# Gate and up of the second layer's FFNs as seven half-size products in place of eight, in three feature groups with partial sums in DRAM

## The chip, the cores and the metric

The kernel runs on one core of one Trainium2 chip. The metric is the device time of one execution in microseconds (us). Engines are named as the profile names them: PE does matrix products (PEld is its weight load), DVE elementwise work, ACT activations, casts and copies, POOL elementwise work and some DMA issues, SP all other DMA issues. Each engine takes its instructions in the order in which the built program has them.

## The reference

Two layers run over 640 tokens of 1024 features (128 of a context, 512 latents), all in float32. A layer is an FFN, a mixer (attention, RG-LRU and S5 branches), and a second FFN, each between two norms whose scale and shift come from a condition (the adaLN vectors):

```python
def _swiglu(h, wg, wu, wd):
    return (jax.nn.silu(h @ wg) * (h @ wu)) @ wd

def _layer(x, mod, lp, ctx):
    s0, c0, g0, s1, c1, g1, s2, c2, g2 = jnp.split(mod, N_MOD, axis=-1)
    h = _rms(x, lp["g_pre"][0]) * (1 + c0) + s0
    f = _swiglu(h, lp["w_ffn_gate"][0], lp["w_ffn_up"][0], lp["w_ffn_down"][0])
    x = x + 0.5 * g0 * _rms(f, lp["g_post"][0])
    ...
    h = _rms(x, lp["g_pre"][2]) * (1 + c2) + s2
    f = _swiglu(h, lp["w_ffn_gate"][1], lp["w_ffn_up"][1], lp["w_ffn_down"][1])
    x = x + 0.5 * g2 * _rms(f, lp["g_post"][2])
```

D_FF is 2816. So an FFN's gate and its up are each a product of 640 x 1024 by 1024 x 2816, its down one of 640 x 2816 by 2816 x 1024. mod = silu(c) @ w_mod + b_mod has 72 blocks of 128 values for a layer and for each of the two conditions.

## The kernel before

The two layers have four FFNs; in the order of the program they are the first and second (layer 0) and the third and fourth (layer 1). Features lie on the partitions for gate and up: a block of 128 features is one step j of 22.

A float32 product is made of three passes over exact parts (`mm3`): the high part of the weights by the high part of the tokens (L93), high by low (L94), low by high (L95). Weights come from DRAM as slabs of 128 x 1024 (`slab`, tile raw, issued by SP). Each half slab is split (`split`): ACT casts it to the high part (L100, tile whi) and DVE subtracts that from the source for the low part (L101, tile wlo). Six such pairs are buffered ahead of PE.

For step j, gate and up each are 8 blocks of the contraction by 3 passes, over 384 tokens and then over 256. Then ACT takes tanh (L433), DVE makes two products out of SBUF and PSUM (L434, L435), and the result is split into the hidden pair (tiles P). After 11 steps (half of the features) down runs over what is there: for each half of the output features, 11 half slabs by 5 token tiles by 3 passes of 512 columns. The first half's sums stay in SBUF (tile part); the second half adds them.

Beside gate and up lies background work at fixed slots of the steps (`plan`, `background`). In the first and the second FFN there are steps that prepare the S5 matrices: the same complex products run on DVE and on POOL (`cmul`, L516 to L524). In all four there are blocks of the adaLN vectors (`mod_tile`): SP brings 128 x 1024 of w_mod, and DVE multiplies and sums it with the two conditions, in halves of 512 columns (L255), with a small sum behind each pair (L258). The first and the third FFN carry 48 such blocks each, the second 24, the fourth 8.

At the end of an FFN each token tile (128 tokens, t = 0 to 4) gets its post norm, its residual and the next pre norm (`post`, `prenorm`). The next norm's scale row is applied before the transposes by DVE (L313, left half) and by ACT and POOL (L314, L315, right half). Then PE transposes (L327), and ACT and DVE add the shift and split (L331 to L338). The tiles 3 and 4 are turned while PE is in the first products of the next phase, which run on the tokens of the tiles 0 to 2.

SP's order is written out in the code; the order on the other engines is set at build time by a scheduler that simulates the program.

## Time and profile before

| | us |
|---|---|
| time, median of 3 runs | 3231.84 (3231.64 to 3232.34) |
| the profiled execution, from first to last instruction | 3232.8 |
| PE busy | 3119.7 (97%) |
| DVE busy | 2008.7 (62%) |
| ACT busy | 1243.2 (38%) |
| POOL busy | 659.9 (20%) |

The profiled execution was taken by itself. Its span is 1.0 us longer than the median of the timed runs, so a time that is worked out within it is compared with the runs by taking 1.0 us off. A busy time is the union of an engine's instructions. PE's matrix products overlap in the records, so the rate of PE is read from the distance between the starts of consecutive ones, not from their lengths. The third FFN runs from about 1664 us to 2112 us of the span, the fourth from about 2756 us to the end.

### The profile page before, as it was taken

What the parts mean: (1) busy time and instruction counts of PE and PEld (TensorE: products, weight loads), DVE (VectorE), ACT (ScalarE), POOL (GpSimd) and SP (SyncE); (2) the same over time, 40 slices, a digit from 0 to 9 for tenths busy, and PEclk for the clock granted to TensorE, in tenths of its full rate; (3) what the DMA queues carried; (4) which work ended last, traced back from release to release, by engine and by line L of the source; (5) the groups of instructions that cost most, each with busy time, mean ns of one, the idle gap of its engine ahead of it and who ended that gap; (6) DMA issues with size and microseconds to landing.
All of it is one profiled execution on the core that took longest, in us unless ns stands there. A gap on an engine that the chain in (4) does not pass through costs nothing.

```text
span 3232.8 us, 52042 instructions
## 1 busy us (share of the span) xinstructions
PE 3119.7 (97%) x19981; PEld 2912.7 (90%) x19981; DVE 2008.7 (62%) x4548; ACT 1243.2 (38%) x2757; POOL 659.9 (20%) x933
## 2 busy tenths in 40 slices
PE   8899999998999999999999999999989999999998
...
GB/s 240 114 181 175 157 157 162 80 80 58 97 140 83 116 133 118 196 98 144 142 152 176 125 112 162 156 113 85 63 67 115 133 72 133 155 85 85 86 98 86
DMA packets 138106, 398.45 MB, mean 123 GB/s; under 512 B 34704, under 2 KB 43424, under 8 KB 135424
## 3 DMA queue, kind: packets, MB, share of 16 engines
...
q10 hardware_dynamic: 720, 1.31, 0.1%
...
HBM read 355.77 MB, written 44.40 MB: 124 GB/s over the span
## 4 chain that ended last, share of the span: by engine, by line
PE 79%; DVE 9%; POOL 6%; issue 3%; ACT 1%; DMA 1%; SPq 0%; POOLq 0%; DVEq 0%; ACTq 0%
PE mm L93 24%; PE mm L94 24%; PE mm L95 24%; POOL s5t L1018 1%; POOL H L1020 1%; POOL s5t L1017 1%; POOL s5t L1019 1%; DVE wlo L101 1%; DVE junk L255 1%; PE mm L1252 1%; DVE x L387 1%; PE mm L1241 1%; PE mm L990 1%; ACT n L310 1%; PE mm L1216 1%
## 5 line engine op out<-in xcount | busy, mean ns | idle before, releaser
L94 PE MATMUL mm<-h,whi 128*128 128x384 f32 (+1 forms) x3968 | 1228.5, 310 | 8.4 <-DVE s L296 5.8
L95 PE MATMUL mm<-h,wlo 128*128 128x384 f32 (+1 forms) x3968 | 1227.2, 310 | 5.8 <-DVE wlo L101 5.8
L93 PE MATMUL mm<-h,whi 128*128 128x384 f32 (+1 forms) x3968 | 1226.2, 311 | 4.5 <-ACT h L337 2.7
L101 DVE TENSOR_TENSOR wlo<-raw,whi 128x512 fp32r<-128x512 f32 x780 | 570.0, 734 | 530.0 <-ACT whi L100 522.6
L94 PEld LDWEIGHTS mm<-h,whi 128*128 128x128 f32 x3968 | 755.9, 191 | 11.4 <-DVE s L296 6.5
L100 ACT CAST whi<-raw 128x512 fp32r<-128x512 f32 x780 | 476.8, 619 | 747.2 <-PE mm L95 367.8
L95 PEld LDWEIGHTS mm<-h,wlo 128*128 128x128 f32 x3968 | 755.7, 191 | 6.9 <-DVE wlo L101 6.8
L93 PEld LDWEIGHTS mm<-h,whi 128*128 128x128 f32 x3968 | 753.9, 191 | 8.7 <-ACT h L337 3.5
L93 PE MATMUL mm<-whi,P 128*128 128x512 f32 x980 | 381.7, 391 | 1.7 <-DVE tmp L434 1.7
L94 PE MATMUL mm<-wlo,P 128*128 128x512 f32 x980 | 381.7, 390 | 0.0
L95 PE MATMUL mm<-whi,P 128*128 128x512 f32 x980 | 381.1, 390 | 0.0
L255 DVE SCALAR_TENSOR_TENSOR junk<-wmod,W 128x512 bf16<-128x512 f32 x512 | 357.7, 699 | 10.3 <-DMA wmod<-w_mod 4.4
L281 POOL DMA_DIRECT2D gd<-grow x6 | 3.2, 528 | 1498.1 <-ACT grow L279 1257.7
L100 ACT CAST P<-tmp 128x384 fp32r<-128x384 f32 x192 | 88.2, 460 | 437.2 <-DVE tmp L435 435.5
L93 PEld LDWEIGHTS mm<-whi,P 128*128 128x128 f32 x980 | 184.0, 188 | 40.4 <-DVE tmp L434 2.2
L95 PEld LDWEIGHTS mm<-whi,P 128*128 128x128 f32 x980 | 184.0, 188 | 38.2
L94 PEld LDWEIGHTS mm<-wlo,P 128*128 128x128 f32 x980 | 184.0, 188 | 37.6
L433 ACT ACTIVATE tmp<-mm 128x384 f32<-128x384 f32 (+1 forms) x176 | 76.4, 435 | 219.8 <-PE mm L95 219.6
L95 PE MATMUL mm<-P,wlo 128*128 128x384 f32 (+1 forms) x512 | 158.8, 310 | 0.0
L94 PE MATMUL mm<-P,whi 128*128 128x384 f32 (+1 forms) x512 | 158.1, 309 | 0.0
L93 PE MATMUL mm<-P,whi 128*128 128x384 f32 (+1 forms) x512 | 158.0, 309 | 0.0
L817 DVE SCALAR_TENSOR_TENSOR tmp<-tmp,mm 128x384 f32<-128x384 f32 x64 | 31.0, 484 | 187.1 <-PE mm L95 94.8
(333 smaller groups left out, 4047.4 us busy)
## 6 DMA issues: line engine op xcount, KB each, us to landing
wmod<-w_mod SPq DMA_DIRECT2D x128, 512.0 KB, 3.6
raw<-w_gate SPq DMA_DIRECT2D x88, 512.0 KB, 3.6
raw<-w_up SPq DMA_DIRECT2D x88, 512.0 KB, 3.6
raw<-w_down SPq DMA_DIRECT2D x88, 512.0 KB, 3.6
raw<-w_in_fm SPq DMA_DIRECT2D x72, 512.0 KB, 3.5
xd<-x SPq DMA_DIRECT2D x25, 512.0 KB, 2.9
x<-xd SPq DMA_DIRECT2D x24, 512.0 KB, 4.5
...
```

What stands on the lines that cost most here:

```text
L93: nc.tensor.matmul(ps, whi, ahi, start=first, stop=False)
L94: nc.tensor.matmul(ps, whi, alo, start=False, stop=False)
L95: nc.tensor.matmul(ps, wlo, ahi, start=False, stop=last)
L100: nc.scalar.copy(hi, src)
L101: return nc.vector.tensor_tensor(lo, src, hi.bitcast(F32), ALU.subtract)
L255: nc.vector.scalar_tensor_tensor(out=jk, in0=w[:, h * 512:(h + 1) * 512], scalar=1.0, in1=rows[c][h], op0=ALU.mult, op1=ALU.mult, accum_ou ...
L310: nc.scalar.activation(n, x, AF.Square, scale=1.0 / 32.0, accum_out=ss)
L387: nc.vector.scalar_tensor_tensor(out=x[:, hs], in0=f[h], scalar=rs, in1=x[:, hs], op0=ALU.mult, op1=ALU.add)
L433: nc.scalar.activation(t, pg[:, :n], AF.Tanh, scale=0.5)
L990: nc.tensor.matmul(pv[:, g], m1[:, g, ri], U[:, 4 * i + g], start=True, stop=True)
L1017: v.tensor_tensor(t[:, 0, :ns], cur, ar, ALU.mult)
L1018: v.tensor_tensor(t[:, 1, :ns], cur[:, :, ::-1], ai, ALU.mult)
```

## The change

In the third and the fourth FFN (`PAIRED`), gate and up work on pairs of steps. Weights of 1024 x 256 are taken as 2 x 2 blocks of 512 x 128, and tokens as two halves of 320 (`TH`). Eight products of half the size become seven (`seven`), with sums of weight blocks, of token blocks and of results in their place:

- Weights: POOL makes four sums of 128 x 512 for a pair and for gate or up (L596). Each of the seven operands is split by ACT and DVE, where four half slabs were split before.
- Tokens: seven operands, kept for the whole FFN in wide tiles (`new_hT`), made once at the boundary before the FFN (`combine`, L364 to L370). The tiles 0, 1 and the first half of 2 give the first two operands; the rest goes into the other five.
- Results: each product of 128 x 320 is copied out of PSUM by ACT or added by DVE (L614, L622, L626, L629, L632). The gate and up values then lie in SBUF, so that DVE's products (L576, L579) have both inputs in SBUF.

A pair of steps has seven products for gate and seven for up. Each is 4 blocks of the contraction by 3 passes over 320 tokens.

The wide tiles take the room in which the hidden pairs and the partial sums lay. So the second, third and fourth FFNs run in three feature groups (`PHASES`), of 6, 8 and 8 steps in the two last. ACT copies a group's down sums out (`put`), and a DMA from POOL's queue writes them to DRAM or adds them there; before the last group's end they are read back (`pd`).

In all FFNs `mod_tile` now sums 1024 columns at once, with one small sum for both conditions. The pre norm's scale is applied with its shift, per feature, after the transposes (`turn`), so POOL has no part in the pre norm any more. The tokens of the condition are computed once.

```diff
-NC_ = 2
-JC = 11
+
+PHASES = {(0, 0): (11, 11), (0, 1): (8, 6, 8), (1, 0): (6, 8, 8), (1, 1): (6, 8, 8)}
+PAIRED = ((1, 0), (1, 1))
+TH = 320
...
-        self.wp = pool("wp", 3)
+        self.wp = pool("wp", 7)
...
-        acc = self.S_(4)
+        m = self.mod[l]["mm"][:, :, col]
         for c in range(2):
-            for h in range(2):
-                jk = self.sm.tile([P, 512], BF16, tag="junk", name=self.nm("junk"), bufs=1)
-                nc.vector.scalar_tensor_tensor(out=jk, in0=w[:, h * 512:(h + 1) * 512], scalar=1.0,
-                                               in1=rows[c][h], op0=ALU.mult, op1=ALU.mult,
-                                               accum_out=acc[:, 2 * c + h:2 * c + h + 1])
-            nc.vector.scalar_tensor_tensor(out=self.mod[l]["m"][c][:, col:col + 1], in0=acc[:, 2 * c:2 * c + 1],
-                                           scalar=acc[:, 2 * c + 1:2 * c + 2], in1=self.mod[l]["b"][:, col:col + 1],
-                                           op0=ALU.add, op1=ALU.add)
...
         rs = self.rstd(ss)
-        self.norm = (
...
-        self.last_n = nc.gpsimd.tensor_tensor(n[:, 512:], n[:, 512:], R["A"][ci][1], ALU.mult)
-        self.turn(t, n, R, hT)
-
...
+    def turn(self, t, n, R, hT):
...
+            for i in range(4):
+                nc.tensor.transpose(ps[:, i * P:(i + 1) * P], n[:, (4 * q + i) * P:(4 * q + i + 1) * P], self.ident)
+            h = n[:, q * 512:(q + 1) * 512].rearrange("p (k t) -> p k t", k=4)
+            for i in range(4):
+                k = slice(4 * q + i, 4 * q + i + 1)
+                o = ps[:, i * P:(i + 1) * P]
+                if i % 2:
+                    v.tensor_scalar(h[:, i], o, a[:, k], b[:, k], ALU.mult, ALU.add)
+                else:
+                    nc.scalar.activation(h[:, i], o, AF.Identity, scale=a[:, k], bias=b[:, k])
+            hs.append(h)
+        if hT.paired:
+            for c, n_, half, o in self.PIECES[t]:
+                d = self.combine(hT, [h[:, :, c:c + n_] for h in hs], half, slice(o, o + n_))
...
+    def combine(self, hT, hs, half, cs):
+        nc, v, g = self.nc, self.nc.vector, self.nc.gpsimd
+        T = {k: (z[:, 0, :, cs], z[:, 1, :, cs]) for k, z in hT.t.items()}
+        if half == 0:
+            self.split(*T["B11"], hs[0])
+            return self.split(*T["B21"], hs[1])
+        h12, h22 = hs
+        n = cs.stop - cs.start
+        f = lambda x: x.bitcast(F32)
+        t1, u = tl(), tl()
+        v.tensor_tensor(t1, f(T["B11"][0]), h12, ALU.subtract)
+        v.tensor_tensor(t1, t1, f(T["B11"][1]), ALU.add)
+        v.tensor_tensor(u, t1, h22, ALU.add)
+        self.split(*T["T1"], t1)
+        g.tensor_tensor(h12, h22, h12, ALU.subtract)
+        g.tensor_tensor(t1, u, f(T["B21"][0]), ALU.subtract)
+        g.tensor_tensor(t1, t1, f(T["B21"][1]), ALU.subtract)
+        self.split(*T["T3"], h12)
+        self.split(*T["T2"], u, -1.0)
+        self.split(*T["B22"], h22)
+        return self.split(*T["T4"], t1)
...
+            h.t = {k: self.wp.tile([P, 2, 4, TH], F32R, tag="W", name=self.nm("h" + k))
+                   for k in ("B11", "B21", "T1", "T3", "T2", "B22", "T4")}
...
+        for ch, n in enumerate(phases):
+            hid = [next(hidden) for _ in range(n)]
...
+                    elif dram:
+                        self.put(t, nh, ps[t], ch)
+                    else:
+                        nc.scalar.copy(part[t][nh], ps[t])
...
+    def put(self, t, nh, ps, ch):
+        nc = self.nc
+        k = (5 * nh + t) % 4
+        o = (self.xp if k % 2 else self.bg).tile([P, 512], F32, tag="x" if k % 2 else "bg", name=self.nm("put"))
+        nc.scalar.copy(o, ps)
+        d = self.pd[t][:, nh * 512:nh * 512 + 512]
+        if ch:
+            nc.gpsimd.dma_start(d, o, accum_op=ALU.add)
+        else:
+            nc.gpsimd.dma_start(d, o)
...
+    def paired(self, l, i, hT):
...
+        big = self.big.tile([P, 5120], F32, tag="big", name=self.nm("raw2"))
+        sets = [[big[:, o:o + 1024], big[:, o + 1024:o + 2048], big[:, o + 2048:o + 2560]] for o in (0, 2560)]
...
+                if jp == 0 and m == 0:
+                    for x in range(2):
+                        ahead[0, x] = opened(0, x)
+                    self.flush()
+                    with ExitStack() as es:
+                        for x in self.norm:
+                            es.enter_context(self.tc.issue_after(x.ins))
+                        ahead[1, 0] = opened(1, 0, True)
+                g, out = ahead.pop((jp, m), None) or opened(jp, m)
+                for done in g:
+                    for f, h in done:
+                        z = out[f][:, h * TH:(h + 1) * TH]
+                        if m == 0:
+                            t = self.tmp.tile([P, 512], F32, tag="tmp", name=self.nm("tmp"))[:, :TH]
+                            nc.scalar.activation(t, z, AF.Tanh, scale=-0.5 if f else 0.5)
+                            v.scalar_tensor_tensor(out=z, in0=t, scalar=1.0, in1=z, op0=ALU.add, op1=ALU.mult)
+                        else:
+                            y = gate[f][:, h * TH:(h + 1) * TH]
+                            v.scalar_tensor_tensor(out=z, in0=z, scalar=0.5, in1=y, op0=ALU.mult, op1=ALU.mult)
+                            self.prod = self.split(*(x[:, h * TH:(h + 1) * TH] for x in hid[f]), z)
+                if m == 0:
+                    gate = out
+                self.background(4 * jp + 2 * m + 1)
+            yield hid[0]
+            yield hid[1]
+
+    def seven(self, src, st, T, out):
+        nc, v, g = self.nc, self.nc.vector, self.nc.gpsimd
+        x, y, s = st
+        nc.sync.dma_start(x, src[:, :1024])
+        self.last_slab = nc.sync.dma_start(y, src[:, 1024:])
+        a11, a12, a21, a22 = x[:, :512], x[:, 512:], y[:, :512], y[:, 512:]
+        add = lambda o, a, b: g.tensor_tensor(o, a, b, ALU.add)
+        o = [[z[:, h * TH:(h + 1) * TH] for h in range(2)] for z in out]
+
+        def product(ps, a, b, more=False):
+            whi, wlo = self.parts(a)
+            for k in range(4):
+                cs = slice(k * P, (k + 1) * P)
+                for e, (w, z) in enumerate(((whi, 0), (whi, 1), (wlo, 0))):
+                    nc.tensor.matmul(ps[:, :TH], w[:, cs], T[b][:, z, k], start=not more and k == e == 0,
+                                     stop=k == 3 and e == 2, skip_group_check=more)
+
+        add(s, a21, a22)
+        add(a21, a21, a11)
+        pa, pb = self.mm(), self.mm()
+        product(pa, a11, "B11")
+        nc.scalar.copy(o[0][0], pa[:, :TH])
+        add(a11, s, a11)
+        product(pb, a12, "B21")
+        v.tensor_tensor(o[0][0], o[0][0], pb[:, :TH], ALU.add)
+        add(a12, a11, a12)
+        yield out
+        yield [(0, 0)]
+        pe, pf = self.mm(), self.mm()
+        product(pe, s, "T1")
+        nc.scalar.copy(o[1][1], pe[:, :TH])
+        product(pf, a21, "T3")
+        v.tensor_tensor(o[1][1], o[1][1], pf[:, :TH], ALU.add)
+        product(pa, a11, "T2", True)
+        nc.scalar.copy(o[0][1], pa[:, :TH])
+        nc.scalar.copy(o[1][0], pa[:, :TH])
+        v.tensor_tensor(o[1][1], o[1][1], pa[:, :TH], ALU.add)
+        yield [(1, 1)]
+        product(pe, a12, "B22", True)
+        v.tensor_tensor(o[0][1], o[0][1], pe[:, :TH], ALU.add)
+        yield [(0, 1)]
+        product(pf, a22, "T4", True)
+        v.tensor_tensor(o[1][0], o[1][0], pf[:, :TH], ALU.add)
+        yield [(1, 0)]
```

The order of instructions shows three places. The first is DVE within the third FFN. Before, in its second half (wlo: the low part of a half slab; tmp: gate or up values, with mm in PSUM; junk: a block of the adaLN vectors):

```order
L435 SCALAR_TENSOR_TENSOR tmp_19941<-tmp_19941,mm_19916 128x256
L258 SCALAR_TENSOR_TENSOR mod_175<-s_19802,bmod_168 128x1
L101 TENSOR_TENSOR wlo_20140<-raw_20133,whi_20139 128x512
L101 TENSOR_TENSOR P_19834<-tmp_19941,P_19833 128x256
L255 SCALAR_TENSOR_TENSOR junk_19950,s_19949<-wmod_19947,W_17541 128x512
L255 SCALAR_TENSOR_TENSOR junk_19952,s_19949<-wmod_19947,W_17541 128x512
L258 SCALAR_TENSOR_TENSOR mod_174<-s_19949,bmod_168 128x1
L255 SCALAR_TENSOR_TENSOR junk_19955,s_19949<-wmod_19947,W_17541 128x512
L434 SCALAR_TENSOR_TENSOR tmp_20045<-tmp_20045,mm_19995 128x384
L255 SCALAR_TENSOR_TENSOR junk_19957,s_19949<-wmod_19947,W_17541 128x512
L258 SCALAR_TENSOR_TENSOR mod_175<-s_19949,bmod_168 128x1
L255 SCALAR_TENSOR_TENSOR junk_19963,s_19962<-wmod_19960,W_17541 128x512
```

After, in its second group of steps (raw_2662: sums of weight blocks; P: gate and up values in SBUF, and their low parts):

```order
L254 SCALAR_TENSOR_TENSOR junk_18760,mod_175<-wmod_18758,srows 128x1024
L579 SCALAR_TENSOR_TENSOR P_18772<-P_18772,P_18613 128x320
L105 TENSOR_TENSOR wlo_18985<-raw_2662_16951,whi_18984 128x512
L254 SCALAR_TENSOR_TENSOR junk_18762,mod_175<-wmod_18758,srows 128x1024
L105 TENSOR_TENSOR wlo_19002<-raw_2662_16951,whi_19001 128x512
L254 SCALAR_TENSOR_TENSOR junk_18767,mod_175<-wmod_18765,srows 128x1024
L254 SCALAR_TENSOR_TENSOR junk_18769,mod_175<-wmod_18765,srows 128x1024
L105 TENSOR_TENSOR wlo_19019<-raw_2662_16951,whi_19018 128x512
L105 TENSOR_TENSOR P_18610<-P_18772,P_18609 128x320
L622 TENSOR_TENSOR P_18773<-P_18773,mm_18820 128x320
L256 TENSOR_TENSOR mod_175<-mod_175,bmod_169 128x2
L105 TENSOR_TENSOR wlo_19041<-raw_2662_16951,whi_19040 128x512
```

Where two splits, a product and a few sums of the adaLN vectors stood between each other, there is now a split at nearly every second place, sums over 1024 columns, and products with both inputs in SBUF. From the first to the last split of this group's weights DVE has 56 splits, 33 additions out of PSUM, 36 products and splits of 320 columns, 24 sums over 1024 columns and 10 small sums; for the third group it is 56, 33, 36, 26 and 11; in the fourth FFN 56, 36, 40, 4 and 2 for either.

The second place is POOL at the start of the third FFN. Before, its last instructions of the norms and then those of the next boundary (s: a norm's root; x: the residual; gd, W: rows of the next boundary):

```order
L300 TENSOR_TENSOR s_17267<-s_17265,mhalf 128x1
L300 TENSOR_TENSOR s_17304<-s_17302,mhalf 128x1
L315 TENSOR_TENSOR n_17262<-n_17262,W_16745 128x512
L390 TENSOR_TENSOR x_17300<-part_14453,x_17300 128x512
L300 TENSOR_TENSOR s_17315<-s_17313,mhalf 128x1
L315 TENSOR_TENSOR n_17310<-n_17310,W_16745 128x512
L281 DMA gd_21509<-grow_21507 32x128
L287 DMA W_21511<-gd_21509 128x2048
```

After (raw, P_17118: sums of weight blocks; n, tc: sums of token blocks):

```order
L596 TENSOR_TENSOR raw_2662_16951<-raw_2662_16951 128x512
L596 TENSOR_TENSOR raw_17116<-P_17118,raw_17116 128x512
L368 TENSOR_TENSOR n_16900<-n_16900 128x512
L596 TENSOR_TENSOR raw_17116<-raw_17116 128x512
L596 TENSOR_TENSOR raw_2662_16951<-raw_2662_16951 128x512
L368 TENSOR_TENSOR n_16943<-n_16943 128x512
L596 TENSOR_TENSOR raw_2662_16951<-raw_2662_16951 128x512
L369 TENSOR_TENSOR tc_17062<-tc_17063,hB_2542_16377 128x512
L370 TENSOR_TENSOR tc_17062<-tc_17062,hB_2542_16377 128x512
L369 TENSOR_TENSOR tc_17098<-tc_17099,hB_2542_16377 128x512
L370 TENSOR_TENSOR tc_17098<-tc_17098,hB_2542_16377 128x512
L596 TENSOR_TENSOR raw_2662_16951<-raw_2662_16951 128x512 x14
```

POOL had nothing to do in the gate and up of the third FFN, and has 88 sums of 128 x 512 there now: 24 in the first group of steps, 32 in each other. The fourth FFN has as many. The sums of a group stand ahead of the writes to DRAM that end the group before, six of them, and behind these the others.

The third place is DVE at the boundary into the third FFN, behind the norm of the last token tile. Before (h: the tokens' parts, wlo: a half slab's low part):

```order
L313 SCALAR_TENSOR_TENSOR n_17310<-x_17300,s_17315,W_16745 128x512
L338 SCALAR_TENSOR_TENSOR h_16660<-mm_17392,mod_175,h_16658 128x128
L101 TENSOR_TENSOR wlo_17447<-raw_17444,whi_17446 128x512
L101 TENSOR_TENSOR wlo_17451<-raw_17444,whi_17450 128x512
L338 SCALAR_TENSOR_TENSOR h_16661<-mm_17405,mod_175,h_16659 128x128
L434 SCALAR_TENSOR_TENSOR tmp_17479<-tmp_17479,mm_17342 128x384
L338 SCALAR_TENSOR_TENSOR h_16661<-mm_17405,mod_175,h_16659 128x128
L435 SCALAR_TENSOR_TENSOR tmp_17479<-tmp_17479,mm_17367 128x384
L338 SCALAR_TENSOR_TENSOR h_16660<-mm_17418,mod_175,h_16658 128x128
```

After (hB and hT: the seven token operands):

```order
L105 TENSOR_TENSOR wlo_17245<-raw_2662_16951,whi_17244 128x512
L365 TENSOR_TENSOR tc_17062<-tc_17062,hB_2541_16376 128x512
L105 TENSOR_TENSOR hB_2546_16381<-n_16900,hB_2546_16381 128x4x128
L614 TENSOR_TENSOR P_17119<-P_17119,mm_17126 128x320
L105 TENSOR_TENSOR hB_2546_16381<-n_16943,hB_2546_16381 128x4x128
L366 TENSOR_TENSOR tc_17063<-tc_17062,n_16900 128x512
L364 TENSOR_TENSOR tc_17098<-hB_2541_16376,n_16943 128x512
L105 TENSOR_TENSOR wlo_17291<-raw_2662_16951,whi_17290 128x512
L105 TENSOR_TENSOR hT_2543_16378<-tc_17062,hT_2543_16378 128x4x128
L105 TENSOR_TENSOR hT_2544_16379<-n_16900,hT_2544_16379 128x4x128
L365 TENSOR_TENSOR tc_17098<-tc_17098,hB_2541_16376 128x512
L108 SCALAR_TENSOR_TENSOR hT_2545_16380<-tc_17063,hT_2545_16380 128x4x128
```

The short instructions of 128 columns became 8, and 16 of 512 columns for the token operands stand between the splits. From the last tile's norm to the last split of the first group's weights DVE has 42 splits, 16 instructions of 512 columns and 8 of 128 for the tokens, 25 additions out of PSUM, 25 products and splits of 320 columns, 18 sums over 1024 columns and 8 small ones. In the fourth FFN it is 42, 16, 8, 26, 28, 4 and 2. POOL has 30 sums there in both: 24 for the weights, 6 for the tokens.

## Rows read from the trace of the kernel before

**Rows 1.** The page's first part: busy time of each engine, share, instructions.
```profile
PE 3119.7 (97%) x19981; PEld 2912.7 (90%) x19981; DVE 2008.7 (62%) x4548; ACT 1243.2 (38%) x2757; POOL 659.9 (20%) x933
```
**Rows 2.** Windows in gate and up: stretch, length, busy by engine, PEclk, DMA, GB/s.
```profile
1680.00:1820.00 140.00, 140.00 (x958) 140.00 (x957) 120.55 (x333) 44.88 (x90) 0.00 (x0) 1.00 0.50 161
1896.00:2040.00 144.00, 144.00 (x972) 143.22 (x971) 111.72 (x298) 43.50 (x85) 0.00 (x0) 1.00 0.46 147
2770.00:2920.00 150.00, 150.00 (x1030) 149.62 (x1030) 78.67 (x170) 49.47 (x102) 0.57 (x1) 1.00 0.30 97
```
**Rows 3.** Timeline of PE, third FFN: start us, us, engine, line, operation, shapes.
```profile
1676.79 0.33 PE L94 MATMUL mm<-h,whi 128*128 128x384 f32 x1
1676.96 0.33 PE L95 MATMUL mm<-h,wlo 128*128 128x384 f32 x1
...
1687.06 0.28 PE L95 MATMUL mm<-h,wlo 128*128 128x256 f32 x1
1687.18 0.28 PE L93 MATMUL mm<-h,whi 128*128 128x256 f32 x1
```
**Rows 4.** Timeline of DVE, first FFN, while POOL does no elementwise work.
```profile
103.09 0.41 DVE L434 SCALAR_TENSOR_TENSOR tmp<-tmp,mm 128x256 f32<-128x256 f32 x1
103.42 0.68 DVE L101 TENSOR_TENSOR wlo<-raw,whi 128x512 fp32r<-128x512 f32 x1
104.02 0.41 DVE L435 SCALAR_TENSOR_TENSOR tmp<-tmp,mm 128x256 f32<-128x256 f32 x1
```
**Rows 5.** Timeline of DVE, third FFN: sums of the adaLN vectors.
```profile
1704.28 0.21 DVE L258 SCALAR_TENSOR_TENSOR mod<-s,bmod 128x1 f32<-128x1 f32 x1
1704.41 0.68 DVE L255 SCALAR_TENSOR_TENSOR junk<-wmod,W 128x512 bf16<-128x512 f32 x1
...
1705.14 0.69 DVE L255 SCALAR_TENSOR_TENSOR junk<-wmod,W 128x512 bf16<-128x512 f32 x1
```
**Rows 6.** Timeline of DVE, first FFN, while POOL does S5 steps.
```profile
95.59 0.54 DVE L435 SCALAR_TENSOR_TENSOR tmp<-tmp,mm 128x384 f32<-128x384 f32 x1
96.05 1.31 DVE L522 SCALAR_TENSOR_TENSOR W<-s5p,W 128x512 f32<-128x512 f32 x1
97.29 1.59 DVE L101 TENSOR_TENSOR wlo<-raw,whi 128x512 fp32r<-128x512 f32 x1
98.80 1.59 DVE L516 TENSOR_TENSOR s5p<-s5p 128x512 f32<-128x512 f32 x1
```
**Rows 7.** Timeline of POOL in the same stretch.
```profile
95.19 1.62 POOL L524 TENSOR_TENSOR W<-s5p,W 128x512 f32<-128x512 f32 x1
96.89 1.44 POOL L516 TENSOR_TENSOR s5p<-s5p 128x512 f32<-128x512 f32 x1
98.29 1.55 POOL L517 TENSOR_TENSOR W<-s5p 128x512 f32<-128x512 f32 x1
```
**Rows 8.** POOL's sum of 128 x 512: ns min/median/max, first and last start us.
```profile
L524 POOL TENSOR_TENSOR W<-s5p,W x16: 1292/1611/1622, 95.2 to 1323.9; 128x512 f32<-128x512 f32 x16
```
**Rows 9.** Windows with S5 steps, and at the boundary into the third FFN.
```profile
100.00:120.00 20.00, 13.41 (x99) 13.01 (x97) 19.95 (x17) 3.32 (x7) 16.63 (x14) 0.94 0.24 83
1220.00:1240.00 20.00, 14.47 (x97) 13.57 (x96) 19.95 (x18) 2.90 (x7) 18.48 (x15) 0.83 0.33 109
1660.00:1670.00 10.00, 5.20 (x21) 3.77 (x20) 9.79 (x18) 6.86 (x15) 5.45 (x5) 0.70 0.51 165
```
**Rows 10.** Timeline of ACT: tanh of gate's last 256 tokens, four steps.
```profile
80.36 0.38 ACT L433 ACTIVATE tmp<-mm 128x256 f32<-128x256 f32 x1
...
238.96 0.37 ACT L433 ACTIVATE tmp<-mm 128x256 f32<-128x256 f32 x1
...
1752.94 0.38 ACT L433 ACTIVATE tmp<-mm 128x256 f32<-128x256 f32 x1
...
2845.35 0.38 ACT L433 ACTIVATE tmp<-mm 128x256 f32<-128x256 f32 x1
```
**Rows 11.** Timeline of DVE: the norm of the last token tile, two boundaries.
```profile
1675.24 0.75 DVE L313 SCALAR_TENSOR_TENSOR n<-x,s,W 128x512 f32<-128x512 f32 x1
...
2767.12 0.75 DVE L313 SCALAR_TENSOR_TENSOR n<-x,s,W 128x512 f32<-128x512 f32 x1
```
**Rows 12.** DMA issues on the page: KB each, median us from issue to landing.
```profile
xd<-x SPq DMA_DIRECT2D x25, 512.0 KB, 2.9
```

More of the change, by code (lines that the diff above doesn't have):

```diff
@@ L278, in rows @@
[L278 to L281 removed]
         out = {}
         if pn:
[L284 to L288 removed]
+            l, ph = pn
@@ L509, in plan @@
             q.setdefault(2 * j + 1, []).append(f)
-        q.setdefault(2 * first + 1, []).insert(0, lambda: self.held(self.silu_rows))
+        if not hasattr(self, "srows"):
+            q.setdefault(2 * first + 1, []).insert(0, lambda: self.held(self.silu_rows))
         self.bgq = q
```

301 lines of the change are left out of this document (173 added, 128 removed).

## The prediction

> **What bounds the kernel now.** I read the page's busy times first. PE is busy for 97% of the span [rows 1], so time that goes must leave PE, and whatever grows elsewhere may grow only as long as PE does not wait for it. The windows come next, by stage. [...] Then the timelines, for the rate at which starts follow each other. On PE that is 0.173 us for 384 columns and 0.12 us for 256 [rows 3]; a step is 48 such pairs, 48 x 0.293 = 14.06 us, and eight steps 112.5. On DVE 256 columns take 0.33 us and 512 take 0.60 [rows 4]; a sum of the adaLN vectors over 512 takes 0.73, the small sum 0.13 [rows 5]. Last I looked for a stretch in which DVE and POOL both work elementwise, because the change makes one. The S5 steps of the first FFN are one. There a DVE instruction of 512 columns with two inputs in SBUF follows the one before at 1.51 us (97.29 to 98.80) instead of 0.60, and POOL's start at the same distance, 95.19, 96.89 and 98.29 [rows 6, 7]. They take turns, one and one. A DVE instruction with one input in PSUM does not pay: the 0.54 us of L435 lies inside POOL's 95.19 to 96.81. In such stretches DVE is full (19.95 of 20) and PE falls to 13.41 of 20, at a granted clock of 0.94, or 14.47 at 0.83 [rows 9].
>
> **The saving on PE.** Before, gate and up of an FFN are 22 x 48 = 1056 pairs of 0.293 us, 309.4 us. After, they are 11 x 14 x 12 = 1848 products of 320 columns. Halfway between 0.12 and 0.173 each takes 0.1465, 270.7 us in all. So 38.7 us of PE work go in each FFN, 77.3 in both. Eight steps take 98.4 us of PE, six 73.8.
>
> [...]
>
> **What DVE gets instead.** By the two pitches 320 columns take 0.40 us on DVE. A sum over 1024 columns takes 0.73 + 0.54 = 1.27 (two steps of 0.27 for 256 more). In the third FFN, group two, from its first to its last split: 56 splits x 0.60 = 33.6; 33 additions out of PSUM x 0.40 = 13.2; 36 products and splits x 0.40 = 14.4; 24 sums x 1.27 = 30.5; 10 x 0.13 = 1.3. Together 93.0 us, less than PE's 98.4. But POOL's 32 sums of weight blocks stand in the same stretch. Each shuts out DVE's instructions with two SBUF inputs, and all but the additions have two now (the products L576 and L579 had one in PSUM before). The price of one POOL sum is what decides the case. Its upper bound is 1.29 us, the shortest that such an instruction takes by itself [rows 8]; its lower bound is nothing, if DVE always had a PSUM instruction or a wait to put beside it. I take 1.51 - 0.60 = 0.91, the row nearest to it, since both are elementwise instructions of 512 columns in a stretch where DVE is full. 32 x 0.91 = 29.1, and DVE needs 122.1 us. It starts early: about six operands are ready when PE comes out of the down product, six splits (3.6 us) and four POOL sums (3.6) that I count off, while the last product (12 x 0.1465 = 1.8) follows the last split. 122.1 - 5.4 = 116.7, against 112.5 before: +4.2. In group three, with 26 and 11 sums, it is 119.4: +6.9.
>
> [...]
>
> Group one starts from the norm of the last token tile [rows 11]. Behind it DVE has 42 splits and 16 instructions of 512 columns for tokens (58 x 0.60 = 34.8), 8 of 128 (0.2 each, 1.6), 50 of 320 (20.0), 18 sums (22.9) and 8 small ones (1.0): 80.3 us. With 30 POOL sums (27.3) and the last product it is 109.4. Before, the sixth step's last tanh started at 1752.94 [rows 10], the last up product was done 24 x 0.12 = 2.9 later, and 1752.94 + 2.9 - 1675.24 = 80.6. So +28.8. The third FFN comes to 28.8 + 4.2 + 6.9 = +39.9.
>
> The fourth FFN carries 4 sums per group instead of 24. Group one: 34.8 + 1.6 + 54 x 0.40 + 5.1 + 0.3 = 63.4 on DVE, + 27.3 + 1.8 = 92.5, against 2845.35 + 2.9 - 2767.12 = 81.1: +11.4. Groups two and three: 33.6 + 36 x 0.40 + 40 x 0.40 + 5.1 + 0.3 = 69.4, + 29.1 = 98.5, as much as PE's 98.4. Two full engines that feed each other lose a little: I take 101, 11.5 less than before in each. Sum 11.4 - 23.0 = -11.6.
>
> **The smaller edits.** A block of the adaLN vectors falls from 4 x 0.73 + 2 x 0.13 = 3.18 us to 2 x 1.27 + 0.13 = 2.67. That counts where DVE is the limit outside the paired FFNs. In the first FFN eight steps with S5 work took 238.96 - 80.36 = 158.6 us [rows 10], 46 over PE's own. About 20 of its 48 blocks lie there: -10 (0 if the scheduler's order leaves them beside waits). The pre norm loses POOL's instruction and one of DVE's on the way to the transposes: -2 at each of the three plain boundaries, -6 (0 to -12, as L313 takes 0.75 [rows 11] and a POOL instruction up to 1.6 [rows 8]). In the four stretches where DVE is the limit some POOL time falls beside the 25 to 33 PSUM additions, 10 to 13 us in each: I take -2 each, -8 (0 to -40). Three FFNs have a group end more, each with a last product that nothing overlaps, 3 x 1.8 = +5. The copies out go to DRAM by DMA from POOL's queue, where the weight sums of the next group stand behind them. I cost that at nothing, because the first six sums stand ahead. If POOL stood still for each of six group ends as long as a transfer to DRAM takes, 2.9 us [rows 12], it would be +17. Two new waits I also cost at nothing. DVE's additions wait for a product that has just ended, with splits for later products behind them; the operands that lie ready cover this (six products of 1.76 us). SP's slabs of a pair wait until one of only two sets of raw tiles is split, and the slabs of w_mod queue behind them; the DMA engines were busy for 0.50 at most [rows 2], so what waits there is made up. If neither held, PE would wait as it does where DVE is full, which is the sum above. ACT's added copies stay small beside its 45 of 140 us [rows 2].
>
> **The sum.** 39.9 - 11.6 - 10 - 6 - 8 + 5 = +9.3. On the profiled execution's 3232.8 that is 3242.1; the median of the runs is 1.0 lower, so 3241 us.
>
> **Rivals.** POOL costs DVE nothing. The third FFN is then bound by PE in groups two and three, 2 x (98.4 - 112.5) = -28.2, and by DVE's 82.1 in group one, +1.5; the fourth by PE everywhere, -28.2 - 10.6. With -11 of small edits the sum is -76, about 3155 us. L435 beside POOL speaks for it, but four of five DVE instructions in group two are no PSUM ones. The 1.51 us speak against.
>
> POOL costs half, 0.45 us, because its sums find DVE's waits and additions. Group one of the third FFN +15.0, two and three -10.5 and -7.8; the fourth -2.4 - 28.2; the small edits -15: -49, about 3183 us. From a price of about 0.83 downwards the kernel gets faster. For it: the wall between the two holds only while DVE has SBUF work at hand.
>
> On the other side, a mechanism that makes it clearly slower: PE, starved by DVE, is granted a lower clock, and then even its shorter work takes longer than before. Rows 9 show 0.83 beside S5 work and 0.70 at the boundary. At 0.83 eight steps take 98.4 / 0.83 = 118.6 us, no more than DVE's 119; below 0.84 the clock decides. At 0.70 they take 140.6 us, +45 for groups two and three of the third FFN, 3286 us; if one group of the fourth falls too, +40 more, 3326. [...] A POOL price of 1.29 ends near by: 124 x 0.38 = 47 and 9 in the fourth, 3297.
>
> That the change doesn't do what it says, seven products for eight, is not a case: the order has them.
>
> **Chances.** The forecast 0.42, with its own range 3220 to 3262. POOL for nothing 0.10, POOL for half 0.22, the clock or the dear POOL 0.26. The range 3175 to 3310 leaves out the first of these and the worst of the last. About 0.2% (6.5 us) is what a measurement of this kernel can tell from no change. Faster takes the two cheap POOL cases and 0.04 of the forecast, 0.36; the same 0.12 of it; slower the rest of it, 0.26, and the last case, 0.52.
>
> **What would show it.** Right: in gate and up of the third FFN DVE near full, POOL busy for about half, PE short of full, splits about 1.5 us apart beside POOL; the first group some 29 us longer than before; in the fourth FFN groups of about 100 us. Products of 320 columns start 0.146 us apart. Wrong: PE full in the third FFN (POOL is free), a granted clock under 0.8 in long stretches, POOL idle ahead of its sums behind the writes to DRAM, or an S5 stretch of the first FFN that stays at 158 us.

## The result, and the profile after

The changed kernel takes 3332.9 us (median of 4 runs, 3330.8 to 3334.9), the kernel before 3231.7 beside it: a ratio of 1.0313, 95% interval 1.0298 to 1.0328. It is slower, as forecast, but by 101 us and not by 9, and outside the range. The profiled execution's span grew from 3232.8 to 3333.2 us.

Page, first part, after (engine, busy us, share, instructions), against [rows 1]:

```profile
PE 3085.1 (93%) x19453; PEld 2862.9 (86%) x19453; DVE 2249.3 (67%) x4266; ACT 1401.8 (42%) x3090; POOL 997.1 (30%) x1190
```

PE's busy time fell by 35 us, and its share with it; DVE gained 241 us and POOL 337. One stretch behind the boundary into the third FFN, then windows in the third's groups two and three and in the fourth's group two (columns as in [rows 2]):

```profile
1700.00:1720.00 20.00, 3.22 (x21) 2.69 (x19) 20.00 (x25) 6.53 (x14) 15.91 (x11) 0.72 0.21 62
...
1860.00:1960.00 100.00, 82.06 (x500) 77.63 (x499) 99.97 (x158) 40.94 (x88) 39.21 (x24) 0.95 0.35 116
2040.00:2140.00 100.00, 82.93 (x513) 77.39 (x512) 99.97 (x157) 40.24 (x87) 39.36 (x23) 0.97 0.34 107
...
3040.00:3100.00 60.00, 60.00 (x411) 60.00 (x410) 59.10 (x91) 33.04 (x71) 27.01 (x18) 1.00 0.31 101
```

In groups two and three of the third FFN DVE is full and PE is not, the reverse of [rows 2]; in the fourth both are full. The first row is the surprise: PE works for 3 of 20 us.

To find the time, I cut both spans at the norm of the last token tile of each boundary [rows 11] and at the last addition of a group's last product. Timeline of DVE, after:

```profile
1685.92 0.76 DVE L310 TENSOR_SCALAR n<-x,s 128x1024 f32<-128x1024 f32 x1
...
1814.00 0.48 DVE L632 TENSOR_TENSOR P<-P,mm 128x320 f32<-128x320 f32 x1
...
1983.82 0.48 DVE L632 TENSOR_TENSOR P<-P,mm 128x320 f32<-128x320 f32 x1
...
2159.61 0.49 DVE L632 TENSOR_TENSOR P<-P,mm 128x320 f32<-128x320 f32 x1
...
2250.38 0.77 DVE L310 TENSOR_SCALAR n<-x,s 128x1024 f32<-128x1024 f32 x1
...
2872.62 0.75 DVE L310 TENSOR_SCALAR n<-x,s 128x1024 f32<-128x1024 f32 x1
...
2979.36 0.47 DVE L632 TENSOR_TENSOR P<-P,mm 128x320 f32<-128x320 f32 x1
...
3120.31 0.47 DVE L632 TENSOR_TENSOR P<-P,mm 128x320 f32<-128x320 f32 x1
...
3275.91 0.48 DVE L632 TENSOR_TENSOR P<-P,mm 128x320 f32<-128x320 f32 x1
```

Stages by these norms (us of the profiled executions; the runs named e... are told below). Between profiles a stage that an edit leaves alone still differs by up to 3 us: the first FFN takes 568.5 to 571.4 in the ten kernels that have the changed one's.

| | first FFN | mixer | second | third | mixer | fourth |
|---|---|---|---|---|---|---|
| before | 565.5 | 615.8 | 493.9 | 475.5 | 616.4 | 465.7 |
| after | 571.4 | 619.9 | 494.6 | 564.5 | 622.2 | 460.6 |
| e1, 7 slabs held back | 570.0 | 619.1 | 494.3 | 542.6 | 621.7 | 460.6 |
| e2, early weights | 569.6 | 619.3 | 496.3 | 555.6 | 622.3 | 453.6 |
| e3, no POOL sums | 570.6 | 619.6 | 495.0 | 492.1 | 620.0 | 446.3 |
| e4, fourth only | 568.5 | 619.3 | 516.4 | 498.4 | 622.2 | 461.8 |
| e6, before + turn | 560.9 | 615.9 | 489.8 | 473.9 | 614.8 | 467.9 |
| e8, e4 + e1 + e2 | 569.0 | 622.8 | 493.6 | 480.3 | 623.9 | 457.8 |
| e10, sums on DVE | 569.3 | 620.3 | 494.3 | 536.5 | 622.3 | 456.4 |
| e13, four edits | 550.3 | 620.1 | 497.5 | 503.2 | 625.5 | 450.2 |
| e14, before + two parts | 548.4 | 615.7 | 488.9 | 474.9 | 614.7 | 467.7 |

Of the 100 us the third FFN has 89. From cut to cut, group one took 128.1 us, the next two 169.8 and 175.8, and the end, up to the next norm, 90.8. These stretches hold the down products too (180 for a group of six steps, 240 for one of eight, 0.227 us each: 40.9 and 54.5 us), and PE begins with a group's down while the last products of the same group still wait:

```profile
1977.87 0.39 PE L97 MATMUL mm<-whi,P 128*128 128x512 f32 x1
1978.10 0.45 PE L604 MATMUL mm<-hB,whi 128*128 128x320 f32 x2
...
1981.01 0.39 PE L97 MATMUL mm<-whi,P 128*128 128x512 f32 x1
```

In the third FFN 50, 65 and 52 down products start ahead of the three cuts (11.3, 14.8 and 11.8 us), in the fourth 19, 18 and 23; before, none did. So the down products that start in a stretch are taken off it below, called net of down. Group one of the third FFN took 116.7 us (before, its six steps 80.6), group two 125.6 and group three 124.3 (before, eight steps 112.5), and the end 48.1 (before 20.3): 36.1, 13.1, 11.8 and 27.8 us more. In the fourth it is 102.4 (before 81.1), 100.3, 100.0 and 8.0.

Two long waits on PE stand at the start of group one (timeline of PE; in brackets the idle time before, and what ended it; hB are the first two token operands, hT the other five):

```profile
1671.36 1.94 PE L327 MATMUL mm<-ident,n 128*128 128x128 f32 x8 [3.50 <-DVE n L310]
...
1687.59 1.43 PE L604 MATMUL mm<-hB,whi 128*128 128x320 f32 x4 [14.29 <-ACT whi L104]
...
1720.52 1.17 PE L604 MATMUL mm<-hT,whi 128*128 128x320 f32 x3 [15.95 <-ACT hT L104]
```

First PE waits for weights. The first pair's slab goes into a wide tile that holds the second FFN's partial sums until their last use, and in SP's order it stands behind the store of the last residual, which waits for the same additions:

```profile
1682.08 0.33 SPq L593 DMA_DIRECT2D raw<-w_pair  x1
```

Then PE waits for the token operands hT; the first product on them starts 34.6 us after the last norm. Only six products (72 instructions on hB) stand before them. DVE is nearly always busy in the group, the time included in which POOL shuts it out: from 1690.59 us on five splits take 8.12 us beside five POOL sums of 8.09 together, where a split takes 0.60 without POOL [rows 4]. Windows of group one in the third and in the fourth FFN:

```profile
1685.92:1814.00 128.08, 97.38 (x570) 91.83 (x571) 124.20 (x190) 55.53 (x114) 54.97 (x34) 0.88 0.38 124
2872.62:2979.36 106.74, 85.91 (x540) 83.45 (x541) 100.11 (x144) 52.85 (x113) 54.41 (x35) 0.89 0.30 99
```

At the end of the third FFN PE has a norm's chain between two tiles' down products:

```profile
2191.53 1.97 PE L327 MATMUL mm<-ident,n 128*128 128x128 f32 x8 [10.69 <-DVE n L310]
2193.15 0.78 PE L97 MATMUL mm<-wr,P 128*128 128x512 f32 x1
...
2208.02 1.97 PE L327 MATMUL mm<-ident,n 128*128 128x128 f32 x8 [7.43 <-DVE n L310]
2209.64 0.78 PE L97 MATMUL mm<-wr,P 128*128 128x512 f32 x1
```

The weights of the second row (wr, a half slab of down held back) had been there since 2163 us; it stands behind the transposes in PE's order.

### The profile page after: what moved, and what is told of

The parts are those of the page before. It is cut to its first block, busy times and chain, and to the rows that moved or that the text cites. A ratio compares the mean times of both kernels' runs of the same rounds, so it can differ in the third digit from the quotient of the medians.

```text
span 3333.2 us, 51703 instructions
## 1 busy us (share of the span) xinstructions
PE 3085.1 (93%) x19453; PEld 2862.9 (86%) x19453; DVE 2249.3 (67%) x4266; ACT 1401.8 (42%) x3090; POOL 997.1 (30%) x1190
## 5 line engine op out<-in xcount | busy, mean ns | idle before, releaser
L99 PE MATMUL mm<-h,wlo 128*128 128x256 f32 (+1 forms) x2560 | 794.1, 311 | 10.3 <-DVE wlo L105 10.2
L97 PE MATMUL mm<-h,whi 128*128 128x256 f32 (+1 forms) x2560 | 794.0, 313 | 9.5 <-ACT W L856 4.7
L98 PE MATMUL mm<-h,whi 128*128 128x256 f32 (+1 forms) x2560 | 794.3, 311 | 0.0
L97 PEld LDWEIGHTS mm<-h,whi 128*128 128x128 f32 x2560 | 488.3, 191 | 13.6 <-ACT W L856 5.3
L99 PEld LDWEIGHTS mm<-h,wlo 128*128 128x128 f32 x2560 | 488.8, 191 | 11.9 <-DVE wlo L105 11.9
L98 PEld LDWEIGHTS mm<-h,whi 128*128 128x128 f32 x2560 | 489.0, 191 | 2.2 <-issue 1.6
L596 POOL TENSOR_TENSOR raw<-raw 128x512 f32<-128x512 f32 x170 | 272.1, 1613 | 371.2 <-DVE wlo L105 187.5
L604 PE MATMUL mm<-hT,whi 128*128 128x320 f32 x1408 | 321.6, 317 | 44.7 <-ACT hT L104 31.9
L254 DVE SCALAR_TENSOR_TENSOR junk<-wmod,srows 128x1024 bf16<-128x1024 f32 x256 | 319.2, 1286 | 5.7 <-DMA wmod<-w_mod 5.6
L604 PEld LDWEIGHTS mm<-hT,whi 128*128 128x128 f32 x1408 | 242.5, 194 | 49.5 <-ACT hT L104 32.4
L604 PE MATMUL mm<-hB,whi 128*128 128x320 f32 x1056 | 238.6, 316 | 41.5 <-ACT whi L104 31.1
L604 PE MATMUL mm<-hT,wlo 128*128 128x320 f32 x704 | 222.3, 318 | 21.0 <-DVE wlo L105 20.8
```

Source lines behind the costliest of these rows:

```text
L97: nc.tensor.matmul(ps, whi, ahi, start=first, stop=False)
L98: nc.tensor.matmul(ps, whi, alo, start=False, stop=False)
L99: nc.tensor.matmul(ps, wlo, ahi, start=False, stop=last)
L254: nc.vector.scalar_tensor_tensor(out=jk, in0=w, scalar=1.0, in1=rows[:, c], op0=ALU.mult, op1=ALU.mult, accum_out=m[:, c:c + 1])
L596: add = lambda o, a, b: g.tensor_tensor(o, a, b, ALU.add)
L604: nc.tensor.matmul(ps[:, :TH], w[:, cs], T[b][:, z, k], start=not more and k == e == 0, stop=k == 3 and e == 2, skip_group_check=more)
```

## The experiments

All ratios are to the kernel before, timed on the same chip. Its median moved between 3230.3 and 3233.2 us from one set of runs to the next, so a difference in us between runs of two sets is good to about 3 us.

| run | median us | ratio (95% interval) |
|---|---|---|
| e1 | 3311.3 | 1.0248 (1.0232 to 1.0263) |
| e2 | 3320.3 | 1.0274 (1.0259 to 1.0289) |
| e3 | 3253.3 | 1.0062 (1.0047 to 1.0077) |
| e4 | 3289.4 | 1.0179 (1.0162 to 1.0196) |
| e5 | 3236.5 | 1.0017 (1.0008 to 1.0026) |
| e6 | 3221.1 | 0.9968 (0.9955 to 0.9980) |
| e7 | 3299.2 | 1.0209 (1.0195 to 1.0224) |
| e8 | 3247.3 | 1.0047 (1.0033 to 1.0062) |
| e9 | 3316.9 | 1.0262 (1.0247 to 1.0278) |
| e10 | 3301.0 | 1.0207 (1.0193 to 1.0221) |
| e11 | 3219.6 | 0.9960 (0.9947 to 0.9972) |
| e12 | 3250.8 | 1.0053 (1.0040 to 1.0067) |
| e13 | 3247.6 | 1.0049 (1.0035 to 1.0063) |
| e14 | 3210.5 | 0.9935 (0.9922 to 0.9947) |
| e15 | 3299.5 | 1.0209 (1.0193 to 1.0225) |

**e1, seven half slabs held back.** At an FFN's end some half slabs of down are kept back. Their products run tile by tile, so that one token tile's norm can run beside the next one's products. `stage` says how many are kept back.

```diff
     def stage(self, n, hT):
-        return n - 1 if hT is not None and hT.paired else n
+        return n - 1
```

> Edit: in the last group of the third FFN seven half slabs of the second output half are held back for the end instead of all eight, so PE's order has the down products of all five token tiles ahead of the first tile's transposes. Theory 'serial end' (each tile's norm chain stands between two tiles' down products on PE): the stretch from the last gate and up product to the next FFN's last norm falls from 90.8 us to about 75, total 3317 us. Rival 'late operands' (PE waits there for the gate rows or for splits, not for the order): same within 3 us, 3330 to 3333 us.

21.6 us less. The end of the third FFN fell from 90.8 to 67.8 us, net of down from 48.1 to 23.6. PE, with the first two tiles' transposes together and behind the down products:

```profile
2201.55 1.03 PE L327 MATMUL mm<-ident,n 128*128 128x128 f32 x8
2203.58 1.03 PE L327 MATMUL mm<-ident,n 128*128 128x128 f32 x8
2215.61 1.94 PE L327 MATMUL mm<-ident,n 128*128 128x128 f32 x8 [10.99 <-DVE n L310]
```

The last group has eight half slabs for each half of the output, and all eight were held back (before, 8 of 11). With none left ahead, the build-time order puts each tile's transposes before the next tile's down; why the scheduler does so was not shown, that it costs 22 us was.

**e2, early weights.**

```diff
-                    for x in range(2):
-                        ahead[0, x] = opened(0, x)
+                    ahead[0, 0] = opened(0, 0, True)
+                    ahead[0, 1] = opened(0, 1)
...
-                        ahead[1, 0] = opened(1, 0, True)
+                        ahead[1, 0] = opened(1, 0)
```

> Edit: the first weight pair of a paired FFN goes into the small raw tiles (the third product into the wide ones), so its DMA need not wait until the partial sums of the mixer's norm leave the wide tile. Theory 'late weights' (PE's 14.3 us wait at the start of the third FFN is the wait for that tile, the DMA and the first splits): 7 to 10 us less at each of two boundaries, 3313 to 3319 us. Rival 'DVE is full in group one anyway': 0 to 4 us less, 3329 to 3333 us.

12.6 us less. PE's first product now waits 3.44 us instead of 14.29, but the wait for the token operands stays:

```profile
1676.34 1.29 PE L604 MATMUL mm<-hB,whi 128*128 128x320 f32 x2 [3.44 <-ACT hB L104]
...
1713.80 1.43 PE L604 MATMUL mm<-hT,whi 128*128 128x320 f32 x4 [13.91 <-ACT hT L104]
```

**e3, no weight sums.** The four `add(...)` lines of `seven` out, `product(pe, s, "T1")` with a21 for s. The kernel leaves out the sums, and its products take unsummed blocks.

> Leaves out POOL's sums of weight blocks in both paired FFNs (their products take the unsummed blocks). Theory 'POOL sum costs DVE 0.91 us' (the prediction's): third FFN, group one 128 to about 106 us, groups two and three from 128.9 and 121.3 to 100 to 104 each; fourth FFN, group one 107 to about 85; total about 3240 us. Rival 'half price': about 3285 us. Rival 'what was lost lies at the boundaries and group ends': above 3300 us.

79.6 us less, somewhat short of the prediction's price. Groups of the third FFN, net of down: 94.6, 100.1 and 101.6 us; the windows of groups two and three have PE nearly full again:

```profile
1830.00:1915.00 85.00, 83.84 (x572) 83.58 (x571) 82.27 (x170) 46.10 (x98) 0.00 (x0) 1.00 0.45 147
1980.00:2070.00 90.00, 88.14 (x595) 86.97 (x594) 86.10 (x177) 48.25 (x102) 0.00 (x0) 1.00 0.50 157
```

Group one stays 14 us over what it was before the change, and in the fourth FFN 10 (91.3 us), without any weight sum on POOL: that is not their doing. In the fourth neither PE nor DVE is full there:

```profile
2797.35:2890.24 92.89, 81.40 (x528) 80.79 (x529) 78.61 (x144) 53.56 (x113) 11.88 (x7) 0.91 0.35 113
```

**e10, the sums on DVE.**

```diff
-        add = lambda o, a, b: g.tensor_tensor(o, a, b, ALU.add)
+        add = lambda o, a, b: v.tensor_tensor(o, a, b, ALU.add)
```

> Edit: the sums of weight blocks on DVE instead of POOL, nothing left out. If a POOL sum costs DVE 0.91 us (prediction), or 0.82 (72 us by 88 sums, from the run without them), 0.60 on DVE is cheaper where DVE is full: 88 x 0.22 to 0.31 = 19 to 27 us less in the third FFN, the fourth's groups two and three unchanged (DVE 69.4 + 19.2 under PE's 98.4), about 3306 to 3314 us. Rival 'POOL's sums run beside DVE's work for a good part, under 0.6': 3335 us and up.

31.9 us less, more than expected: 28.0 in the third FFN. DVE does 88 more instructions of 0.60 us there and is done sooner, so a POOL sum had cost it 0.60 + 28.0/88 = 0.92 us on average (1.03, 0.98 and 0.76 by group, net of down). In the changed kernel the price can be seen in a row: a split with two SBUF inputs takes 1.64 us beside a POOL sum, an addition out of PSUM 0.47 inside one.

```profile
1698.64 0.47 DVE L614 TENSOR_TENSOR P<-P,mm 128x320 f32<-128x320 f32 x1
...
1946.55 1.64 DVE L105 TENSOR_TENSOR wlo<-raw,whi 128x512 fp32r<-128x512 f32 x1
```

POOL in the same stretches:

```profile
1698.12 1.73 POOL L596 TENSOR_TENSOR P<-raw 128x512 f32<-128x512 f32 x1
...
1946.37 1.27 POOL L596 TENSOR_TENSOR raw<-raw 128x512 f32<-128x512 f32 x1 [8.29 <-DVE wlo L105]
```

**e15, half of the adaLN sums in the third FFN.** For layer 1's columns 16 to 63, `in0=w[:, :512]`, `in1=rows[:, c, :512]`; the kernel leaves out the other half of each sum.

> The changed kernel with the adaLN sums of the third FFN over half of their columns (leaves out the other half). DVE is at the limit there by the prediction: 18 + 24 + 26 wide sums at 1.15 us become 0.61, 37 us of DVE work less; groups two and three can fall to PE's 98 to 102 us, 20 to 26 and 18 to 20 us less, group one 5 to 10 us less, in all 35 to 45 us: 3288 to 3298 us. Rival 'the splits wait for POOL's sums and for the weights, not for DVE': under 15 us less.

33.4 us less (net of down, group one 7.7, two 12.2, three 11.1), nearly all of the 37 us of DVE work. Groups two and three of the third FFN had been 25 and 24 us above the fourth's 100; half of the adaLN sums makes nearly half of that. That the other half makes the rest is likely by this, but not shown. Without the other load on DVE, POOL's sums (e3), the same groups fall to 100.1 and 101.6, near PE's own time, with all adaLN sums in place. So it takes both loads.

**e9, no token sums.** `combine` splits h12 and h22 as they are into the five operands; the kernel leaves out their sums.

> Leaves out the sums of token blocks at the two paired boundaries (the five operands are split from the unsummed blocks, as many splits as before). Theory 'group one is a chain of latencies: norm, transposes, sums in turn on DVE and POOL, splits, and PE has only six products to put beside it': the first product of the other five operands starts 34.6 us after the last norm now, 24 to 28 us then, 14 to 20 us less in all, 3313 to 3319 us. Rival 'DVE's sum of work sets group one, as the prediction had it': 12 us of DVE and POOL work less (8 x 0.60 and 6 x 0.91) only in the third FFN, 5 or less in the fourth; the start of that product hardly earlier.

16.0 us less, 6.0 and 8.3 of it in the two paired FFNs. The first product on the other operands starts 29.8 us after the norm instead of 34.6:

```profile
1684.74 1.44 PE L595 MATMUL mm<-hB,whi 128*128 128x320 f32 x4 [15.19 <-ACT whi L104]
...
1710.41 1.42 PE L595 MATMUL mm<-hT,whi 128*128 128x320 f32 x3 [8.95 <-ACT hT L104]
```

The total is as the chain had it, that start later than it had it. It does not settle chain against sum: the rival took DVE to have room in the fourth FFN, and the window of group one has DVE busy there, too, for 100.1 of 106.7 us. What else holds the start is, by e2, e10 and e3 (28.6, 30.9 and 25.8 us), the weights' delay and POOL's sums in the same queues; none removes it alone.

**e4 and e8, only the fourth FFN with seven products.** `PAIRED = ((1, 1),)`, and for e8 the edits of e1 and e2.

> Edit: only the fourth FFN has the seven products; the third has plain gate and up, in three groups of features with partial sums in DRAM. Theory 'the third FFN's 89 us come from DVE with POOL and from its boundary': third FFN back to about 478 us from last norm to last norm, total about 3245 us, fourth FFN as it was (-5 us against before). Rival 'three groups and their writes to DRAM cost the third FFN by themselves': 15 us or more over that, 3260 us and up.

> Only the fourth FFN with seven products, the third plain in three groups; seven half slabs held back; the first weight pair of the fourth FFN in the small raw tiles. Theory 'the 44 us that the third FFN lost without seven products are two serial ends (second and third FFN)': 44 us less than without these edits, and 7 for the early weights, about 3238 us. Rival 'writes to DRAM and groups cost it': 3265 us and up.

e4 missed: 3289 and not 3245. The second FFN's end, now without paired tokens behind it, had all eight slabs held back as well:

```profile
1648.28 1.97 PE L327 MATMUL mm<-ident,n 128*128 128x128 f32 x8 [7.35 <-DVE n L310]
...
1665.02 1.97 PE L327 MATMUL mm<-ident,n 128*128 128x128 f32 x8 [7.43 <-DVE n L310]
1681.03 1.94 PE L327 MATMUL mm<-ident,n 128*128 128x128 f32 x8 [8.12 <-DVE n L310]
```

e8 took both ends away and the weights' wait, 42 us, and came to 3247 (9 over its expectation). In both, plain gate and up of a group of eight take 112.6 us up to the first down product, as before, so the writes to DRAM cost nothing there. e12 below, with two groups for three, has the second and third FFN 2.7 and 1.3 us shorter than e8.

**e7, e1 and e2 together.**

> Both edits together: seven half slabs held back, and the first weight pair in the small raw tiles. If the serial end of the third FFN and the late weights at the boundaries are separate losses (21 and 13 us by themselves), the sum: about 3298 us. If they share a wait: 3305 to 3311 us.

3299.2: the two are separate losses and add up.

**e5, e11 and e6, parts of the change on the kernel before.** e5 has the new `mod_tile`; e11 also starts the blocks later:

```diff
-            self.plan(..., modq(l, range(16, 64)), 0 if l else 3)
+            self.plan(..., modq(l, range(16, 64)), 0 if l else 6)
```

> The kernel before with one edit: the sums of the adaLN vectors over 1024 columns at once, one small sum for both conditions. Theory of the prediction (fewer and cheaper DVE instructions where DVE is full beside the S5 steps): 10 us less, about 3222 us, gate and up of the first FFN's first half end near 225 us of the span. [...]

> The kernel before with the wide sums, and the first FFN's 48 blocks of adaLN sums start at step 6 instead of 3. Theory 'the wide sum is cheaper, but the order set at build time then puts more blocks (16.5 for 12.5) into the half in which DVE is full with S5 steps': with fewer blocks there it is faster than before, 3220 to 3227 us. Rival 'a longer instruction lets POOL and DVE take turns worse': 3232 to 3238 us.

e5 is 6.2 us slower than the kernel before, e11 13.6 us faster. The windows of the first FFN up to its first down product, for DVE's adaLN instructions alone (length, busy us and count, then PEclk, DMA and GB/s; nearly half of the count reads the accumulator), before,

```profile
54.00:238.00 184.00, 42.66 (x105) 0.94 0.45 149
```

in e5,

```profile
52.00:243.00 191.00, 48.39 (x71) 0.94 0.46 156
```

in e11,

```profile
52.00:225.00 173.00, 23.64 (x37) 0.96 0.44 149
```

and after:

```profile
55.00:245.00 190.00, 49.18 (x70) 0.93 0.46 156
```

That is 53 sums of 512, 13 blocks, before; 36 of 1024, 18 blocks, in e5 and after; 20, 10 blocks, in e11. The block got cheaper (42.66/13.25 = 3.2 us busy before, 48.39/18 = 2.7 in e5), and the order set at build time put five more of them into the half in which DVE is full.

> The kernel before with one edit: the pre norm's scale applied with its shift after the transposes, POOL out of the pre norm. Theory of the prediction (one POOL and one DVE step less on the way to the transposes): 2 us less at each of four boundaries, 3224 to 3226 us. Rival 'eight short steps of 128 columns, in turn on ACT and DVE, and then whole splits are a longer chain than before': 3 to 5 us more at each boundary, 3240 to 3250 us.

e6 (`rows`, `prenorm` and `turn` as in the change, one wide tile for the gate rows) is 9.1 us faster, 3 us more than the prediction had.

**e12, two groups for the plain FFNs.** e8 with `PHASES` (11, 11) for the second and third FFN and 512-column sums.

> Only the fourth FFN with seven products and three groups; the second and third FFN plain in two halves as before, seven half slabs held back, first weight pair in the small raw tiles, adaLN sums over 512 columns again. Sum of what the runs showed: 3247 with three groups and wide sums, 6 less for the narrow sums, 8 less for two groups (third FFN 480 to 474, second 494 to 490): 3231 to 3235 us. Rival 'the mixers' 7 us each go with the groups too': about 3220 us, faster than before.

A miss: 3250.8. The narrow sums came to 64 ahead of the first down product, 16 blocks, and the first FFN to 572.8 us; the mixers stayed 4 and 8 us over before (619.8 and 624.8). What in the change makes the mixers longer stays open.

**e13, four edits at once; e14, the parts that gain, on the kernel before.** e13 is the change with the edits of e1, e2, e10 and e11's later start; e14 is e6 with e11.

> The changed kernel with four edits together: seven half slabs held back, first weight pair in the small raw tiles, weight sums on DVE, adaLN blocks of the first FFN from step 6. By themselves they gave 21.6, 12.6, 31.9 and (on the kernel before) 16.9 us. If these are separate causes they add up: 3333 - 83 = 3250 us, and the first FFN's last norm moves from 571 to about 553 us. If they overlap in the third FFN (DVE's sums and the late weights both act on group one): 3258 to 3268 us.

> The kernel before with the two parts of the change that gain by themselves: the scale after the transposes, and the wide adaLN sums with their blocks from step 6. If they are separate (9.1 and 13.6 us): 3208 to 3211 us, faster than both kernels. If both act on DVE in the same stretch: 3214 to 3219 us.

e13: 3247.6, 85.3 less than the change; the sum of the four was 83.0. So the four losses are separate and add up. e14: 3210.5 us, 0.65% faster than the kernel before (21 us), and the fastest of all.

## Why the prediction was wrong

The direction was right, and so was the mechanism named for the middle of an FFN: DVE is full in groups two and three of the third and pays for POOL's sums. The sum was not: +9 where 100 were measured, and the range ended at 3310. Its terms one by one, in us of the span, the measured ones net of down:

| term | predicted | measured | shown by |
|---|---|---|---|
| third FFN, group one | +28.8 | +36.1 | e2, e3, e9 |
| groups two, three | +4.2, +6.9 | +13.1, +11.8 | e3, e10, e15 |
| third FFN's end | none named | +27.8 | e1 |
| fourth FFN, group one | +11.4 | +21.3 | e2, e3, e9 |
| groups two, three | -11.5 each | -12.2, -12.5 | |
| first FFN | -10 | +5.9 | e5, e11 |
| mixers and second FFN | -6 (boundaries) | +10.6 | e6 in part |
| group ends | +5 | fourth FFN's last -2 | |
| PSUM overlap | -8 | not seen by itself | |

**The rates held.** PE's 320 columns: three starts in 0.44 us, 0.147 each, against 0.1465 predicted.

```profile
1960.17 0.46 PE L604 MATMUL mm<-hB,whi 128*128 128x320 f32 x2
1960.46 0.31 PE L604 MATMUL mm<-hB,wlo 128*128 128x320 f32 x1
1960.61 0.46 PE L604 MATMUL mm<-hT,whi 128*128 128x320 f32 x2
```

The price of a POOL sum, "what decides the case", was 0.91 and came out at 0.92 (e10) or 72.4/88 = 0.82 (third FFN of e3, where PE becomes the limit). Groups of the fourth FFN were predicted at 101 us and took 100.3 and 100.0.

**The step that cost most is a part of the program that I left out**: the end of the third FFN, for which the sum has no term. It grew by 27.8 us. That `rest` now holds back all of a group's slabs, and that PE's order has there a tile's transposes between 24 down products and the next 24, stood in the order of instructions; the prediction follows that order only at the boundary into the FFN. e1 took 21.6 us off.

**The second is group one**, in the two paired FFNs 17 us more than the +28.8 and +11.4 that I had for it. I added up DVE's instructions and POOL's sums from the last norm on as if DVE were full from there and PE's wait did not count. But PE has only 10.6 us of products to lay beside the 35 us until the other token operands are there, and DVE, though nearly full, stands idle for 3.9 us in the third FFN and 6.6 in the fourth. Even without POOL's weight sums (e3) group one takes 94.6 and 91.3 us, where my terms give 80.3 + 1.8 + 6 x 0.91 = 87.6 and 70.7. In the fourth FFN of e3 DVE is idle for 14 of 93 us, so there it is a path that counts: weights that come late, then transposes, sums in turn on DVE and POOL, and splits. I had the order that shows it (16 instructions of 512 columns between the splits) and read it as a sum. Each of e2 and e9 took 6 to 7 us off either group one; how the rest divides between such waits and DVE's work stays open.

**The third is the first FFN.** I took the number of blocks in the full stretch as fixed (20) and their saving as 0.51 us each. They were 13 and became 18, for a gain of 10 a loss of 3 to 6. The saving was mis-sized too. The 0.73 us for a sum of 512 [rows 5] holds where another sum follows, with the reading of the accumulator in between; where a split follows, on the kernel before, the starts are 0.61 apart, and a sum of 1024 in e5 takes 1.15 and not 1.27, also where another follows.

```profile
126.76 0.68 DVE L255 SCALAR_TENSOR_TENSOR junk<-wmod,W 128x512 bf16<-128x512 f32 x1
...
127.37 0.68 DVE L101 TENSOR_TENSOR wlo<-raw,whi 128x512 fp32r<-128x512 f32 x1
```

```profile
124.53 1.22 DVE L254 SCALAR_TENSOR_TENSOR junk<-wmod,W 128x1024 bf16<-128x1024 f32 x1
...
125.68 1.22 DVE L254 SCALAR_TENSOR_TENSOR junk<-wmod,W 128x1024 bf16<-128x1024 f32 x1
```

**The mixers and the second FFN** took 10.6 us more where I had 6 less. e6 shows the gain at the boundaries (9.1 us on the kernel before); what takes it away in the changed kernel stays open.

**Of the rivals**, the clock did not decide: PE's granted clock in the third FFN's groups two and three is 0.95 and 0.97. The dear POOL, 1.29 us for each of 124 sums (94 in the third FFN, 30 in the fourth's group one), did not come either: in the third FFN a sum cost 0.92 (e10) or 0.82 us (e3) on average. The two cheap POOL cases were wrong. Groups two and three of the third FFN are 8.9 and 4.9 us over their forecasts, about as much as if the lead of 5.4 us at a group's start were not there; no run shows that lead, or the 8 us beside PSUM additions, by itself. That the writes to DRAM cost nothing held, to within 3 us an FFN (e4, e8, e12). DVE's new wait cost nothing within the groups, since DVE is full (99.97 of 100 us in groups two and three of the third FFN, 59.10 of 60 in the fourth's group two); SP's late slab mattered at the boundary (e2), where I had no term for it.
